# A decoder trunk on one core: the first input projection in two passes of four k-tiles, silu(c) without its last copies, half of the first squares on VectorE

## The chip, the cores and the metric

The kernel runs on one core of one Trainium2 chip. The metric is the device time in microseconds (us) of one execution; less is better. The engines that matter are TensorE (PE in the profile; its weight loads are PEld), VectorE (DVE), ScalarE (ACT) and the queue of SyncE (SPq), from which nearly all transfers are issued. Each engine has its own list of instructions, written by a scheduler when the kernel is built.

## What is computed

Two layers of a hybrid decoder for 256 tokens of width 2048, all in float32. The part that matters here is the start: the conditioning c goes through silu and a large matrix and gives, for each layer, shifts, scales and gates; x is normed and modulated with them, and the first (even) layer projects the result to 5120 columns.

```python
cond = jax.nn.silu(c.astype(F32))
for layer in range(DEPTH):
    mod = cond @ ada_w[layer].astype(F32) + ada_b[layer].astype(F32)
    sh1, sc1, g1, sh2, sc2, g2 = jnp.split(mod, 6, axis=-1)
    h = modulate(rmsnorm(x, norm_mix[layer]), sh1, sc1)
    if layer % 2 == 0:
        y = even_mixer(h, positions, ...)      # proj = h @ w_in, then attention and RG-LRU
    else:
        y = odd_mixer(h, positions, ...)
    x = x + (g1[:, None] * y.astype(F32)).astype(x.dtype)
    ...                                        # gated conv FFN, in the same way
return rmsnorm(x, norm_final)
```

`modulate` is h * (1 + scale) + shift.

## The kernel before

Activations are held transposed, as 16 k-tiles of 128 features by 256 tokens. Weights stream from HBM through six buffers of 128x2048 (`w`, also used by the modulation columns), in one queue.

**Products.** For float32 accuracy a weight tile is split: ScalarE casts it to the rounded `hi` (L379 in `slab`, L330 in `pieces`), VectorE subtracts and gives `lo` (L380, L331); there are four buffers of each. The activation is split in the same way, and a product is three: hi by high, hi by low, lo by high. A native form without a split exists as well (`full` in `slab`).

**Modulation.** `ada_tile` (L217) loads one 128x2048 piece of the matrix and reduces it with cond on VectorE (L221): one column of 128 shifts or scales. A k-tile needs two. `modulator` (L298) asks for them in `tile_of` (`ada_upto`), finishes scale and shift by two tiny operations (L310, L311), multiplies x by scale and norm (L289, VectorE), and adds the shift on ScalarE (L291 for the high half, L293 for the native tile), then VectorE makes the low half (L294). Besides the columns that are asked for, `ada_fill` adds columns by a quota after each slab. The columns have a lower priority than other work of the scheduler (`U_ADA`).

**Norm.** `rms` (L258) squares the 16 tiles on ScalarE (L264), sums them by products with ones, and takes root (L280) and reciprocal (L284). silu(c) is made in four pieces of 512: a product that spreads c, tanh (L210, ScalarE), a product on VectorE (L211) and a copy times 0.5 (L212, ScalarE).

**The first projection.** Three slabs, ev_a (v and part of q and k: 7 banks of PSUM), ev_b (7 banks) and ev_c (6 banks), each run by `run` in `slab_set` (L488) over k-tiles 0 to 7; ev_a is native there. As there are eight banks, a slab's banks are copied away by ScalarE (L506) before the next can use them. Then ev_a goes over k-tiles 8 to 15 (L719) and its banks are added on VectorE to what was copied (L509); the rest of ev_b and ev_c, k-tiles 8 to 15, comes in groups of 256 columns (`ev_rest`, L720 on; products of `group`), added in L517. The quotas in `EV_FIRST` (L40) are the columns per k-tile for the three slabs.

Of the kernel before, what the change touches and what calls it, by code (L numbers as in the profile page):

```python
# [14 lines left out]
AF = mybir.ActivationFunctionType  # L15
# [4 lines left out]
D = 2048  # L20
# [19 lines left out]
EV_FIRST = (0.0, 0.6, 1.0)  # L40
# [55 lines left out]
def trunk(ctx: ExitStack, tc: tile.TileContext, a: dict, out: bass.AP):  # L96
# [54 lines left out]
    def pin():  # L151
        """the next product comes after all the products before it"""
        pinned[0] = PIN

    def start(chain, prio=0):
        """a chain of work whose parts go between pieces of the weight stream"""
        chains.append((chain, prio))
        advance(chains[-1])
# [15 lines left out]
    # ---------------------------------------------------------------- inputs that are needed first  # L174
# [28 lines left out]
    # silu(c), the same row on all partitions  # L203
    cond = cst.tile([P, D], F32, name="cond")
    for h in range(4):
        c = slice(h * 512, (h + 1) * 512)
        ps = pss()
        mm(ps, ones[0:1, :], crow[:, c], True, True)
        th = t2()
        S.activation(th, ps, AF.Tanh, scale=0.5)  # L210
        V.scalar_tensor_tensor(th, th, 1.0, ps, op0=ALU.add, op1=ALU.mult)  # L211
        S.activation(cond[:, c], th, AF.Copy, scale=0.5)  # L212

    # ---------------------------------------------------------------- adaLN: one column of 128 at a time
    mods = [cst.tile([P, 96], F32, name=f"mods{l}") for l in range(2)]

    def ada_tile(l, j):  # L217
        w = sb.tile([P, D], F32, tag="w", name=nm("ada"), bufs=WB)
        DMA.dma_start(w, a["adaT"][l, j])
        with urgent(U_ADA):  # L220
            V.tensor_tensor_reduce(out=w, in0=w, in1=cond, scale=1.0, scalar=0.0, op0=ALU.mult,  # L221
                                   op1=ALU.add, accum_out=mods[l][:, j:j + 1])
# [19 lines left out]
    def gate_of(l, q):  # L242
        """gate(i): columns i and i + 1 of a gate"""
# [13 lines left out]
    # ---------------------------------------------------------------- norm  # L257
    def rms(on_pe=False, warm=(0, 0)):  # L258
        """1 / sqrt(mean(x^2) + eps); warm: products that only keep the array's clock up, before the sum and after"""
        ps = pss()  # L260
        acc = None
        for i in range(KT):
            sq = t1()
            S.activation(sq, x[i], AF.Square)  # L264
# [33 lines left out]
    def modulator(l, q, g, on_pe=False):  # L298
        """h[i](): the i-th k-tile of the normed and modulated x; q: the chunk of the shift"""
# [21 lines left out]
    # ---------------------------------------------------------------- weight streams  # L321
# [13 lines left out]
    def group(srcs, acts):  # L335
        """out^T of 256 columns: [128, 2, T] in one bank; srcs: (chunk, k-tiles)."""
# [18 lines left out]
    def group_f32(src, acts):  # L355
        """the same, with float32 operands that are not split"""
# [10 lines left out]
    def slab(src, n, xa, first, last, pv, pg, full=None):  # L367
        """one k-tile of n columns: of v (token-major: pv[2 * half + block]) and of groups of 256"""
# [14 lines left out]
        def product(o, wide, cs, bs, st):  # L383
            """wide: the weights are the moving operand"""
# [19 lines left out]
    def step(emit, post, quota, when=False, prio=0):  # L404
        """a group's products come before the last group's results are used"""
# [19 lines left out]
    def out_proj(name, g0, gate, acts, quota, chunked=False, base=None):  # L425
        """x += gate * (acts @ W) for all 2048 columns; chunks from g0 on.
        Without a gate x becomes the product alone; with a base it holds such a product, and base the old x."""
# [37 lines left out]
    # ---------------------------------------------------------------- sin and cos of an angle  # L465
# [6 lines left out]
    def sin_cos1(sn, cm, ang):  # L472
        """sn = sin(ang), cm = cos(ang) - 1; ang in [-pi, pi]"""
# [4 lines left out]
    # ---------------------------------------------------------------- start: ada of layer 0, tables  # L478
# [9 lines left out]
    def slab_set(specs, tile_of):  # L488
        """specs: (name, columns, banks of v, groups); run(si, k0, k1, ..): the k-tiles k0..k1 of one of them"""
# [22 lines left out]
        def rest(si, g, k0, post, quota):  # L512
            """group g of a slab without v: its k-tiles from k0 on"""
# [14 lines left out]
    for si in range(3):  # L528
        ev_slab(si, 0, HALF, EV_FIRST[si], si == 0)
# [17 lines left out]
    def rope(o, src, tab, half, by_dma=False):  # L547
        """o, src: [128, n, T]"""
# [14 lines left out]
    # softplus(-lambda) = max(-lambda, 0) + log1p(exp(-|lambda|))  # L563
# [24 lines left out]
    # ---------------------------------------------------------------- S5: what the parameters give  # L588
# [11 lines left out]
    # ---------------------------------------------------------------- attention  # L600
# [41 lines left out]
    # ================================================================ layer 0: mixer  # L642
# [24 lines left out]
    def lru1(i, x2, xin):  # L667
        """gates of tile i; x2: (b, t, a) in the making"""
# [71 lines left out]
    # ================================================================ FFN  # L740
# [64 lines left out]
    # ================================================================ layer 1: mixer  # L805
# [88 lines left out]
    def s5_load(g, ps):  # L894
        """two tiles of u: rows (t, 32 channels) -> (q, 32 channels)"""
# [12 lines left out]
    def turn_rows(src, dst, g):  # L908
        """[128 (a, 32), m, b, c] -> [128 (b, 32), m, a, c]"""
# [15 lines left out]
    def s5_all():  # L925
        """tile i's tables, tile i - 1's states and tile i - 2's outputs, side by side"""
# [63 lines left out]
    # ================================================================ last norm  # L990
# [9 lines left out]
# -------------------------------------------------------------------- S5  # L1000
# Chunks of 4 tokens; 64 chunks. In a chunk, with A = exp(lam dt) and Bb = ((A - 1) / lam) B:
#   v_c = sum_j A^(3-j) Bb u_(4c+j),  H_c = A^4 H_(c-1) + v_c,
#   y_(4c+j) = Re(C A^(j+1) H_(c-1)) + sum_(d<=j) Re(C A^d Bb) u_(4c+j-d) + D u_(4c+j).
# H is scanned in a frame that turns with A^4, where the decay is real.
# [344 lines left out]
```

## Time and profile before

| | |
|---|---|
| time, median of 3 runs | 2273.1 us |
| lowest and highest run | 2271.8 and 2273.46 us |
| span of the profiled execution | 2271.8 us |
| TensorE busy | 2209.5 us (97%) |
| VectorE busy | 1812.8 us (80%) |
| ScalarE busy | 1221.4 us (54%) |
| HBM | 269 GB/s over the span |

The profiled execution's own time is its span. A busy TensorE means that a product is in the pipe; a product's row also holds its way through the array, so rows of a stream overlap, and the distance from start to start tells what one costs. The same holds, with less overlap, for VectorE. "Idle before" names what ended an engine's idle time just before an instruction.

### The profile page before, as it was taken

The numbers are of one execution on the slowest core, as the hardware profiler recorded it, in microseconds if no ns is written. First come the engines' busy times: TensorE is split into PE (matmuls) and PEld (weight loads), VectorE is DVE, ScalarE is ACT, GpSimd is POOL, SyncE is SP. The second block draws the span as 40 slices with busy tenths as digits, with TensorE's granted clock in tenths as the row PEclk, the third lists the DMA queues.
The fourth block names the chain that finished last, engine by engine and source line by source line (L and its number), as shares of the span: only waits on it lengthen the run. The fifth ranks groups of instructions, "written<-read, shape, count | busy, mean of one in ns | idle before, by whom it ended". The sixth has DMA issues, their size and how long they took to land. (4 is left out here: it accounts for less than half of the span.)

```text
span 2271.8 us, 42923 instructions
## 1 busy us (share of the span) xinstructions
PE 2209.5 (97%) x17498; PEld 2148.6 (95%) x17498; DVE 1812.8 (80%) x2908; ACT 1221.4 (54%) x2056; POOL 4.4 (0%) x12
## 2 busy tenths in 40 slices
PE   7999999998999999999999999999999999999997
PEld 4899989898999999999999899999999999999997
DVE  7789989989998869989778778986888657666655
ACT  3355856444775456654445767644565434544543
POOL 0000000000000000000000000000000000000000
PEclk9999999999999999999999999999999999999998
DMA  9988689888669778888866665967756667655541
GB/s 349 373 337 308 235 303 350 333 327 338 259 242 352 306 295 317 320 336 314 304 238 224 245 254 224 342 222 289 276 181 222 238 244 287 234 185 180 203 181 69
DMA packets 106088, 615.43 MB, mean 271 GB/s; under 512 B 12065, under 2 KB 14625, under 8 KB 54817
## 3 DMA queue, kind: packets, MB, share of 16 engines
q1 hardware_dynamic: 105890, 612.69, 71.9%
q8 instruction: 137, 2.24, 0.4%
q14 instruction: 61, 0.50, 0.1%
HBM read 592.72 MB, written 18.87 MB: 269 GB/s over the span
## 5 line engine op out<-in xcount | busy, mean ns | idle before, releaser
L138 PE MATMUL mm<-t,hi 128*128 128x256 f32 x9568 | 1744.2, 284 | 7.3 <-ACT hi L379 4.3
L138 PEld LDWEIGHTS mm<-t,hi 128*128 128x128 f32 x9568 | 1498.5, 193 | 10.4 <-ACT hi L379 4.7
L138 PE MATMUL mm<-t,lo 128*128 128x256 f32 x4784 | 1356.7, 284 | 5.1 <-DVE lo L331 5.1
L138 PEld LDWEIGHTS mm<-t,lo 128*128 128x128 f32 x4784 | 919.8, 192 | 7.3 <-DVE lo L331 5.8
L330 ACT CAST hi<-w 128x1024 fp32r<-128x1024 f32 (+1 forms) x558 | 565.4, 1016 | 594.4 <-PE mm L138 523.2
L331 DVE TENSOR_TENSOR lo<-w,hi 128x1024 fp32r<-128x1024 f32 (+1 forms) x558 | 657.5, 1182 | 280.2 <-ACT hi L330 276.3
L221 DVE CUSTOM_DVE_ANT_0 ada<-ada,cond 128x2048 f32<-128x2048 f32 x192 | 438.3, 2283 | 22.7 <-DMA ada<-in_adaT 19.7
L379 ACT CAST hi<-w 128x768 fp32r<-128x768 f32 (+2 forms) x160 | 146.4, 921 | 163.1 <-PE sx L138 86.6
L380 DVE TENSOR_TENSOR lo<-w,hi 128x768 fp32r<-128x768 f32 (+2 forms) x160 | 167.4, 1061 | 62.3 <-ACT hi L379 61.6
L138 PE MATMUL sp<-t,hi 128*128 128x256 f32 x832 | 153.6, 283 | 0.0
L138 PEld LDWEIGHTS sp<-t,hi 128*128 128x128 f32 x832 | 130.3, 192 | 0.8 <-ACT hi L379 0.2
L138 PE MATMUL sp<-t,lo 128*128 128x256 f32 x416 | 117.1, 283 | 0.0
L759 DVE SCALAR_TENSOR_TENSOR t<-mm,ffn_p,t 128x255 f32<-128x255 f32 x232 | 110.6, 477 | 4.2 <-ACT t L757 1.7
L138 PEld LDWEIGHTS sp<-t,lo 128*128 128x128 f32 x416 | 79.6, 192 | 0.1
L291 ACT ACTIVATE t<-t,mods 128x256 fp32r<-128x256 f32 x64 | 30.0, 505 | 85.6 <-DVE mods L311 62.8
L138 PE MATMUL sx<-t,t 128*128 128x64 f32 (+2 forms) x480 | 68.3, 283 | 3.3 <-DMA t<-s 1.1
L757 ACT ACTIVATE t<-mm,ffn_p 128x256 f32<-128x256 f32 x116 | 65.0, 560 | 5.6 <-DVE t L759 5.4
L138 PEld LDWEIGHTS sx<-t,t 128*128 128x128 f32 x480 | 61.5, 194 | 5.9 <-issue 3.3
L264 ACT ACTIVATE t<-x 128x256 f32<-128x256 f32 x80 | 31.9, 414 | 59.4 <-DVE x L451 31.9
L138 PE MATMUL mm<-t,w 128*128 128x256 f32 x256 | 56.5, 379 | 0.9 <-ACT t L665 0.9
L138 PEld LDWEIGHTS mm<-t,w 128*128 128x128 f32 x256 | 48.5, 190 | 7.8 <-ACT t L665 1.3
L318 ACT CAST t<-t 128x256 fp32r<-128x256 f32 x102 | 40.2, 402 | 26.1 <-DVE t L763 20.1
(264 smaller groups left out, 1475.1 us busy)
## 6 DMA issues: line engine op xcount, KB each, us to landing
ada<-in_adaT SPq DMA_DIRECT2D x192, 1024.0 KB, 6.5
w<-in_ffn_in SPq DMA_DIRECT2D x116, 1024.0 KB, 6.1
w<-in_ffn_out SPq DMA_DIRECT2D x80, 896.0 KB, 4.7
w<-in_ffn_first SPq DMA_DIRECT2D x48, 896.0 KB, 6.6
w<-in_ev_out SPq DMA_DIRECT2D x16, 1024.0 KB, 6.4
w<-in_ffn_out SPq DMA_DIRECT2D x16, 1024.0 KB, 5.2
w<-in_od_out SPq DMA_DIRECT2D x16, 1024.0 KB, 7.4
w<-in_ev_a SPq DMA_DIRECT2D x16, 896.0 KB, 7.0
```

The source lines that it names most:

```text
L138: keep(PE.matmul(o, l, r, start=start, stop=stop, skip_group_check=True))
L221: V.tensor_tensor_reduce(out=w, in0=w, in1=cond, scale=1.0, scalar=0.0, op0=ALU.mult, op1=ALU.add, accum_out=mods[l][:, j:j + 1])
L264: S.activation(sq, x[i], AF.Square)
L291: S.activation(o[:, 0, :], t, AF.Identity, bias=sh[:, i:i + 1])
L318: S.copy(o[:, 0, :], src)
L330: S.copy(hi[:, :m], w[:, o:o + m])
L331: V.tensor_tensor(lo[:, :m], w[:, o:o + m], hi[:, :m].bitcast(F32), op=ALU.subtract)
L379: S.copy(hi[:, :c], w[:, o:o + c])
L380: V.tensor_tensor(lo[:, :c], w[:, o:o + c], hi[:, :c].bitcast(F32), op=ALU.subtract)
L757: S.activation(c, ps[:, s, :], AF.Identity, bias=fp[:, 3, j:j + 1], scale=fp[:, 2, j:j + 1])
L759: V.scalar_tensor_tensor(c[:, d:], ps[:, s, :T - d], fp[:, 2 - d, j:j + 1], c[:, d:], op0=ALU.mult, op1=ALU.add)
```

## The change

The three slabs go over k-tiles 0 to 3 first, and then, in a second round, over 4 to 7. In `run` a slab that doesn't start at k-tile 0 adds its banks on VectorE (L511 in the changed kernel, which is L509 here), so the second round adds 20 banks; the number of copies on ScalarE stays 20. Only k-tiles 0 to 3 of ev_a are native now (`si == 0 and k0 == 0`). The quotas are 0, 1, 1 columns per k-tile in the first round and 0.6 in the second. The copy times 0.5 behind silu(c) goes away and the 0.5 goes into the reduction of the columns. The squares of odd tiles of the first norm are made by VectorE. All else in the difference are comments that are left out and lines that move by two or three.

```diff
-EV_FIRST = (0.0, 0.6, 1.0)
+EV_FIRST = ((0, 4, (0.0, 1.0, 1.0)), (4, 8, (0.6, 0.6, 0.6)))
...
         S.activation(th, ps, AF.Tanh, scale=0.5)
-        V.scalar_tensor_tensor(th, th, 1.0, ps, op0=ALU.add, op1=ALU.mult)
-        S.activation(cond[:, c], th, AF.Copy, scale=0.5)
...
+        V.scalar_tensor_tensor(cond[:, c], th, 1.0, ps, op0=ALU.add, op1=ALU.mult)
...
-            V.tensor_tensor_reduce(out=w, in0=w, in1=cond, scale=1.0, scalar=0.0, op0=ALU.mult,
+            V.tensor_tensor_reduce(out=w, in0=w, in1=cond, scale=0.5, scalar=0.0, op0=ALU.mult,
                                    op1=ALU.add, accum_out=mods[l][:, j:j + 1])
...
         for i in range(KT):
             sq = t1()
-            S.activation(sq, x[i], AF.Square)
+            if on_pe and i % 2:
+                V.tensor_tensor(sq, x[i], x[i], op=ALU.mult)
+            else:
+                S.activation(sq, x[i], AF.Square)
...
-    for si in range(3):
-        ev_slab(si, 0, HALF, EV_FIRST[si], si == 0)
+    for k0, k1, quotas in EV_FIRST:
+        for si in range(3):
+            ev_slab(si, k0, k1, quotas[si], si == 0 and k0 == 0)
```

Three places of VectorE's list show what moves. In the names, ada is a piece of the modulation matrix, mods the columns, x the four blocks of x, sp and sm small parameters, t a tile. An ada row is followed by a row that reads its sum out into mods.

The first excerpt is VectorE at the start, ahead of the first column. Before:

```order
L211 SCALAR_TENSOR_TENSOR t_8_101<-t_8_101,sp_99 128x512
L580 TENSOR_SCALAR sp_1281<-sp_1281 128x8
L1026 TENSOR_SCALAR sm_1316<-sm_1316 128x32
L1027 SCALAR_TENSOR_TENSOR sm_1315<-sm_1316,pack 128x32
L1028 SCALAR_TENSOR_TENSOR sm_1315<-sm_1316,sm_1315 128x32
L1029 TENSOR_SCALAR sm_1315<-sm_1315 128x32
L1030 TENSOR_SCALAR sm_1316<-sm_1316 128x32
L1031 CAST sm_1317<-sm_1316 128x32
L221 ISA ada_171,mods_105<-ada_171,cond 128x2048
L221 ISA mods_105 128x1
```

and after the change:

```order
L1031 SCALAR_TENSOR_TENSOR sm_1440<-sm_1441,sm_1440 128x32
L575 TENSOR_TENSOR sp_1407<-sp_1405,sp_1408 128x8
L1032 TENSOR_SCALAR sm_1440<-sm_1440 128x32
L576 TENSOR_TENSOR sp_1408<-sp_1407 128x8
L264 TENSOR_TENSOR t_25_149<-x_73 128x256
L577 TENSOR_SCALAR sp_1405<-sp_1408 128x8
L1033 TENSOR_SCALAR sm_1441<-sm_1441 128x32
L579 TENSOR_TENSOR sp_1405<-sp_1405,sp_1408 128x8
L1034 CAST sm_1442<-sm_1441 128x32
L220 ISA ada_167,mods_101<-ada_167,cond 128x2048
```

The last product of silu(c) (L211) stood eight rows ahead of the first column and now stands further ahead; the square of the last tile (L264 here) stands five rows ahead of the column.

The second excerpt is VectorE in the last eight k-tiles of ev_a. Before, one column stands behind the weights of k-tile 12 and the low half of k-tile 14's activation (t_277_1753):

```order
L311 TENSOR_TENSOR mods_105<-mods_105,pack 128x1
L289 SCALAR_TENSOR_TENSOR t_276_1751<-x_73,A_160,t_27_158 128x256
L380 TENSOR_TENSOR lo_1662<-w_1659,hi_1661 128x1024
L380 TENSOR_TENSOR lo_1666<-w_1659,hi_1665 128x768
L294 SCALAR_TENSOR_TENSOR t_277_1753<-t_276_1751,mods_105,t_277_1753 128x256
L221 ISA ada_1699,mods_105<-ada_1699,cond 128x2048
L221 ISA mods_105 128x1
L310 SCALAR_TENSOR_TENSOR A_160<-mods_105,b_29_161,pack 128x1
L289 SCALAR_TENSOR_TENSOR t_284_1801<-x_73,A_160,t_27_158 128x256
L303 TENSOR_SCALAR b_639_4006<-pack 128x16
```

and after the change three columns stand in a row behind the weights of k-tile 11 and ahead of the low half of its activation (t_281_1731):

```order
L382 TENSOR_TENSOR lo_1737<-w_1734,hi_1736 128x1024
L382 TENSOR_TENSOR lo_1741<-w_1734,hi_1740 128x768
L220 ISA ada_1677,mods_101<-ada_1677,cond 128x2048
L220 ISA mods_101 128x1
L220 ISA ada_1774,mods_101<-ada_1774,cond 128x2048
L220 ISA mods_101 128x1
L313 TENSOR_TENSOR mods_101<-mods_101,pack 128x1
L220 ISA ada_1777,mods_101<-ada_1777,cond 128x2048
L220 ISA mods_101 128x1
L296 SCALAR_TENSOR_TENSOR t_281_1731<-t_280_1729,mods_101,t_281_1731 128x256
```

From here to k-tile 15 two columns stand ahead of each modulated tile, nine in all; before, four were spread over the eight k-tiles.

The third excerpt is VectorE at the end of these k-tiles, where the additions of ev_a's banks (mm, sx, sp) and the first chunk of ev_b's rest meet. Before, the low half of the chunk's first part (lo_1857) stands ahead of the additions:

```order
L294 SCALAR_TENSOR_TENSOR t_285_1803<-t_284_1801,mods_105,t_285_1803 128x256
L380 TENSOR_TENSOR lo_1809<-w_1806,hi_1808 128x1024
L380 TENSOR_TENSOR lo_1813<-w_1806,hi_1812 128x768
L331 TENSOR_TENSOR lo_1857<-w_1854,hi_1856 128x1024
L509 TENSOR_TENSOR t_85_386<-mm_1451,t_85_386 128x512
L331 TENSOR_TENSOR lo_1861<-w_1854,hi_1860 128x1024
L509 TENSOR_TENSOR t_86_387<-mm_1452,t_86_387 128x512
L509 TENSOR_TENSOR t_87_388<-mm_1453,t_87_388 128x512
```

and after the change it (lo_2000) stands behind all of them and behind a column:

```order
L382 TENSOR_TENSOR lo_1953<-w_1946,hi_1952 128x768
L511 TENSOR_TENSOR t_61_274<-mm_1576,t_61_274 128x512
L220 ISA ada_1986,mods_101<-ada_1986,cond 128x2048
L220 ISA mods_101 128x1
L511 TENSOR_TENSOR t_62_275<-mm_1577,t_62_275 128x512
L511 TENSOR_TENSOR t_63_276<-mm_1578,t_63_276 128x512
L511 TENSOR_TENSOR t_64_277<-sx_1579,t_64_277 128x512
L511 TENSOR_TENSOR t_65_278<-sp_1580,t_65_278 128x512
L511 TENSOR_TENSOR t_66_279<-sp_1581,t_66_279 128x512
L511 TENSOR_TENSOR t_67_280<-sp_1582,t_67_280 128x512
L333 TENSOR_TENSOR lo_2000<-w_1997,hi_1999 128x1024
```

What moved is the low half of the next weights: from ahead of the first addition to behind the seventh.

## Rows read from the trace of the kernel before

**Rows 1.** Section 1 of the page: busy us (share of the span) xinstructions.

```profile
PE 2209.5 (97%) x17498; PEld 2148.6 (95%) x17498; DVE 1812.8 (80%) x2908; ACT 1221.4 (54%) x2056; POOL 4.4 (0%) x12
```

**Rows 2.** By stretch: us, busy PE, PEld, DVE, ACT, POOL; PEclk; DMA share; GB/s.

```profile
25.10:34.40 9.30, 9.28 (x21) 5.15 (x22) 8.83 (x45) 4.03 (x7) 0.00 (x0) 0.67 0.94 348
51.10:59.00 7.90, 7.89 (x21) 4.54 (x22) 7.22 (x10) 0.91 (x2) 0.00 (x0) 0.78 0.93 364
84.10:124.40 40.30, 40.30 (x337) 40.27 (x336) 29.29 (x33) 19.06 (x25) 0.00 (x0) 1.00 0.93 352
124.40:159.30 34.90, 34.88 (x291) 34.68 (x289) 30.69 (x42) 14.11 (x21) 0.00 (x0) 1.00 0.96 382
159.30:202.70 43.40, 39.83 (x240) 35.43 (x241) 38.26 (x55) 22.05 (x31) 0.00 (x0) 1.00 0.81 310
202.70:242.70 40.00, 39.79 (x328) 39.36 (x327) 39.26 (x83) 28.54 (x47) 0.00 (x0) 1.00 0.63 225
...
160.30:196.00 35.70, 33.12 (x195) 29.22 (x196) 33.08 (x48) 18.20 (x27) 0.00 (x0) 1.00 0.80 312
```

**Rows 3.** Timeline of PE: start, us, line, operation, count, [idle before <- what ended it].

```profile
25.12 5.49 PE L138 MATMUL mm<-w,t 128*128 128x512 f32 x6 [5.42 <-ACT t L293]
...
51.11 4.54 PE L138 MATMUL mm<-w,t 128*128 128x512 f32 x6 [2.99 <-ACT t L293]
...
58.94 2.74 PE L138 MATMUL mm<-w,t 128*128 128x512 f32 x6
...
64.96 2.74 PE L138 MATMUL mm<-w,t 128*128 128x512 f32 x6
```

**Rows 4.** Groups of VectorE, 16 to 200 us: count | busy us, mean ns | idle before.

```profile
L221 DVE CUSTOM_DVE_ANT_0 ada<-ada,cond 128x2048 f32<-128x2048 f32 x32 | 73.1, 2284 | 3.9 <-ACT cond L212 2.8 <-DMA ada<-in_adaT 1.1
...
L294 DVE SCALAR_TENSOR_TENSOR t<-t,mods,t 128x256 fp32r<-128x256 f32 x16 | 7.5, 480 | 7.3 <-ACT t L291 7.3
...
L470 DVE SCALAR_TENSOR_TENSOR t<-t,t 128x256 f32<-128x256 f32 x3 | 1.2, 416 | 0.0
```

**Rows 5.** Timeline of VectorE, single rows from 13 to 203 us.

```profile
13.39 0.18 DVE L1031 CAST sm<-sm 128x32 int32<-128x32 f32 x1
16.39 2.29 DVE L221 CUSTOM_DVE_ANT_0 ada<-ada,cond 128x2048 f32<-128x2048 f32 x1 [2.82 <-ACT cond L212]
...
50.69 0.48 DVE L294 SCALAR_TENSOR_TENSOR t<-t,mods,t 128x256 fp32r<-128x256 f32 x1 [0.57 <-ACT t L291]
...
132.93 1.83 DVE L380 TENSOR_TENSOR lo<-w,hi 128x1024 fp32r<-128x1024 f32 x2
...
160.34 0.48 DVE L294 SCALAR_TENSOR_TENSOR t<-t,mods,t 128x256 fp32r<-128x256 f32 x1 [3.85 <-ACT t L291]
...
169.60 4.09 DVE L380 TENSOR_TENSOR lo<-w,hi 128x1024 fp32r<-128x1024 f32 x4
...
195.01 0.95 DVE L380 TENSOR_TENSOR lo<-w,hi 128x768 fp32r<-128x768 f32 x1
...
202.27 1.87 DVE L509 TENSOR_TENSOR t<-sp,t 128x512 f32<-128x512 f32 x3
```

**Rows 6.** Timeline of ScalarE: the last copy of silu(c).

```profile
15.75 0.61 ACT L212 ACTIVATE cond<-t 128x512 f32<-128x512 f32 x1
```

**Rows 7.** Timeline of PE where ev_a's last k-tiles begin, and where the next chunk does.

```profile
161.69 1.65 PE L138 MATMUL mm<-hi,t 128*128 128x512 f32 x6 [2.41 <-ACT hi L379]
...
202.74 0.40 PE L138 MATMUL mm<-t,hi 128*128 128x256 f32 x2
202.98 0.28 PE L138 MATMUL mm<-t,lo 128*128 128x256 f32 x1
```

**Rows 8.** DMA issues, 0 to 200 us: count, KB each, median us to landing.

```profile
ada<-in_adaT SPq DMA_DIRECT2D x34, 1024.0 KB, 6.8
...
w<-in_ev_b SPq DMA_DIRECT2D x8, 896.0 KB, 7.9
w<-in_ev_c SPq DMA_DIRECT2D x8, 768.0 KB, 6.2
```

## The prediction

> **What bounds the kernel now.** I read first the busy line of the page: TensorE works 97% of the span and VectorE 80% [rows 1]. So what the change gives must come from TensorE work that disappears or from the 3% in which TensorE waits, and what it costs can come from VectorE becoming late. Second, the table by stretch [rows 2]: from 84.1 to 159.3 TensorE is full; the stretch from 159.3 to 202.7, in which the last eight k-tiles of ev_a run, has a hole of 3.6 us. VectorE is the other full engine: 8.83 of 9.30 us near the start, 38.26 of 43.40 in the last eight k-tiles, 39.26 of 40 after that. Third, the start on TensorE [rows 3]: k-tile 0 begins at 25.12 behind a wait of 5.42, k-tile 3 at 51.11 behind 2.99, both for ScalarE's modulated tile; from k-tile 4 at 58.94 the native float32 k-tiles follow each other every 6.02 us, and ev_b begins at 84.1. Fourth, what VectorE does there [rows 4, 5]: 32 modulation columns ("ada", 2.28 us each, two per k-tile), the low halves of the split weights, and the modulated tiles. The first column starts at 16.39, and the last operation for k-tile 3 at 50.69; the table shows hardly any idle time between. So k-tile 3 waits for VectorE's list, not for TensorE.
>
> **The sum goes by VectorE's list.** VectorE works its instructions off in the order in which they stand, so I follow that list from the first column to the weights of ev_b's rest. The three excerpts of the order are the fixed points, and TensorE waits where it must.
>
> **Start.** Removed: four copies of silu(c) on ScalarE; the last starts at 15.75, takes 0.61 us, and the first column starts behind it at 16.39 [rows 5, 6]. Added: eight squares on VectorE. No row of before shows one; the nearest are operations on 128x256 of 0.42 to 0.48 us [rows 4, 5]. They don't put 8 x 0.45 on the path, since VectorE stood idle for 2.82 us ahead of 16.39, but the last square waits until TensorE's sum has read the eighth, and it stands nearly directly ahead of the first column (first excerpt). I take the first column at 15.2; the bounds are 13.6, when the small operation of 13.39 is done, and 16.4. From there to k-tile 3 the list has 113 instructions where 119 stood, tiny ones at 0.1 us: 0.5 less. So k-tile 3 starts at about 51.1 - 1.7 = 49.4, and ends at 57.2 if it takes 7.8 us as before (51.11 to 58.94), of which 1.8 are the lower clock.
>
> **The two passes on TensorE.** K-tiles 4 to 7 of ev_a leave the native form: 6.02 us each [rows 3] become three products of split halves, which take 41.05 / 8 = 5.1 us, short waits included (161.69 to 202.74) [rows 7]. That is the gain: 3.7 us. An ev_b tile is 40.3 / 8 = 5.04 us and an ev_c tile 34.9 / 8 = 4.36 [rows 2]. Behind k-tile 3 follow 20.2 (ev_b), 17.4 (ev_c), 20.4 (ev_a), 20.2 and 17.4: 95.6 us, to 152.8 without a wait. I add three waits. ScalarE has five evictions ahead of the first cast of ev_c: 0.3. In ev_c's first pass two tiles take VectorE 2 x (2.3 + 1.8) for columns and low halves [rows 4, 5] and 0.8 to 1.0 for the modulation, 9.0 to 9.2, against 8.7 on TensorE: 1.1 in all. From ev_c to ev_a the first cast stands behind the last eviction and one modulation, 0.6 + 0.5 + 1.0 = 2.1, close to the 2.41 that the trace shows at a border of the same kind [rows 7]. Together 156.3, where 159.3 stood: 3.0 us earlier.
>
> The second pass adds its banks on VectorE instead of copying them on ScalarE: 20 additions of some 0.62 us [rows 5], 12.4 us of new VectorE work, and four k-tiles of ev_a now need low halves, 4 x 2.0 = 8 [rows 5]. The first two borders hide this: a bank is finished several products before the next slab wants it, and VectorE's list for a slab of four tiles (halves 8, additions 4.3, two or three columns 4.6 to 6.9) sums to 17 to 19 us against 20. At the third border VectorE is late by itself: going through its list I find it done with ev_c's six additions at 157.4. Before, the same point (the first low half of an activation of the last eight tiles) is 160.34 [rows 5].
>
> **The last eight k-tiles of ev_a.** Here the sign is decided. All 32 columns must be done by k-tile 15, before and after. Before, 16 are done in the first ev_a, 12 more by the quotas 0.6 x 8 + 1.0 x 8, and 4 stand in this stretch. After: 8, then 1.0 x 8 = 8, then 0.6 x 12 = 7; 9 are left to stand here (second excerpt: three of them ahead of one low half). VectorE's list of before takes 160.3 to 196.0, 35.7 us, of which 33.1 are busy [rows 2, 5]. After: 35.7 + 5 x 2.3 (columns) + 0.4 (one more product with the norm) + 0.7 (rope's angle, partly done earlier before) + 0.5 (five tiny operations) + 1.7 (three more waits of 0.57 for ScalarE, like the one at 50.69) - 1.5 (waits for casts, which are no longer last) = 49.0 us. TensorE needs 41. The list ends at 157.4 + 49.0 = 206.4, where before it ends at 195.01 + 0.95 = 196.0.
>
> Behind it the order changes once more (third excerpt). Before, the low half of the next chunk stands ahead of the additions, and TensorE goes on at 202.74 without a hole. After, there come an addition, a column, six additions and only then that low half: 0.6 + 2.3 + 3.7 + 1.2 = 7.8. The first product with it starts at 214.2, against 202.98 [rows 7]: **11.2 us later**. TensorE's last k-tile, 205 to 210, or to 212 at a lower clock, hides in that.
>
> Beyond it the list is the same. By the output projection 40 columns are done in both, so one column less (2.3 us) stands in a stretch in which TensorE loses 0.2 us of 40 [rows 2]; I give it nothing (bounds 0 and -2.3). The profiled execution spans 2271.8 us, which is also the lowest of the three runs; the median is 2273.1. On the span the sum gives 2283.0, on the median **2284.3 us**.
>
> **Clock.** Two waits in the start are followed by half speed: behind the 5.42 us before k-tile 0 the granted clock is 0.67 over 25.1 to 34.4, and the tile takes 9.3 instead of 6.02; behind the 2.99 us before k-tile 3 it is 0.78, and the tile takes 7.8; behind 2.41 us at 159.3 it stays at 1.00 [rows 2, 3, 7]. In the last eight tiles I expect TensorE to wait about 5 us in tile 11 and 3 to 4 us in 14 and 15. The loss would be 3.3 + 1.8 + 1.8 = 6.9 if nothing hid it; since what follows waits for VectorE anyway I count 0, and keep 6.9 for the range. The Trainium skill, "TensorE: Matmul & The Clock Gate", section "HAM oscillation — how this bites in real kernels", speaks against the change: it advises to run all k-tiles of an output in one go, since waits between the pieces let the clock fall. By it the 6.9 would be paid in full; the drops at 25.1 and 51.1 agree that waits do this, and no run here shows whether a late VectorE hides the price.
>
> **Rivals.** *Faster*: TensorE alone decides. It is 3.0 us ahead at the end of ev_c, 6.5 if the three waits don't come, and the stretch costs 43.4 as before: 2266 to 2270, say 2268. For it: TensorE is 97% busy and loses 3.7 us of work. Against it: VectorE's list would have to fit in the some 41 us of the stretch, so it decides at one or two columns more than the four of before; the order has five more. 5%. *No change*: the passes run better than I count: no waits (-3.5), full clock in k-tile 3 (-1.8), first column at 13.6 (-1.6). The last list then starts near 151 and ends near 200; about +4, 2277. 10%. *Worse*: DMA and clock. The first pass behind k-tile 3 needs 8 columns of 1024 KB, 4 tiles of 896 and 4 of 768 [rows 8], 15.2 MB, in 37.6 us: 404 GB/s, where the stretches show 348 to 382 [rows 2]; at 382 it takes 2.2 us more, at 352 5.6. With part of the 6.9 of clock: +14 to +23, say 2291. 14%. That the forecast holds (2280 to 2289): 71%.
>
> **How the numbers follow.** A difference of 0.2%, 4.5 us, is about what can be told from none. Faster by that: 5%. Within it: the middle rival and an edge of the forecast, 11%. Slower: 84%. The range takes in most of the two slower rivals: 2276 to 2294.
>
> **What would show it.** Right: TensorE finishes k-tile 3 at 55 to 58 and the passes at 154 to 158; the last eight tiles of ev_a take 50 us or more, with TensorE waiting for low halves of activations or weights while VectorE has no idle time and nine columns there; the first products of ev_b's rest wait for their low half behind the additions. Wrong: VectorE with idle time in that stretch, a start of the last eight tiles before 150, or TensorE waits there that end with a DMA.

## The result and the profile after

The changed kernel takes 2284.8 us (median of 4 runs, 2279.6 to 2291.9) against 2272.45 us for the kernel before on the same chip: a ratio of 1.0055, 95% interval 1.0032 to 1.0078. It is slower by about 12 us, by the interval 7 to 18; the prediction said 2284.3. The profiled execution is the fastest of the four: span 2277.9, time 2279.64 us, 1.7 us above its span. The 2271.8 us of the profiled execution of the kernel before is a span as well, so the 2277.9 is to be compared with it: 6.1 us more.

The busy line of the page, answering to [rows 1]: TensorE is busy 1.7 us longer, VectorE 21.5.

```profile
PE 2211.2 (97%) x17538; PEld 2152.1 (94%) x17538; DVE 1834.3 (81%) x2944; ACT 1222.5 (54%) x2048; POOL 4.4 (0%) x12
```

The table by stretch of the changed kernel, with the columns of [rows 2]: the first k-tile, k-tile 3, the last eight k-tiles of ev_a with the wait behind them, and the 40 us after that.

```profile
25.60:34.40 8.80, 8.72 (x20) 4.87 (x21) 8.13 (x30) 3.85 (x7) 0.00 (x0) 0.69 0.80 292
52.40:58.30 5.90, 5.90 (x19) 3.72 (x20) 1.90 (x3) 4.46 (x8) 0.00 (x0) 1.00 0.88 333
156.70:213.00 56.30, 45.46 (x244) 38.05 (x242) 54.01 (x78) 19.37 (x28) 0.00 (x0) 0.94 0.90 337
213.00:253.00 40.00, 39.53 (x322) 38.96 (x323) 39.23 (x80) 27.03 (x44) 0.00 (x0) 1.00 0.69 243
```

The third row is where the time goes: 56.3 us, where before 43.4 stood, with VectorE busy for 54.0 of them and TensorE for 45.5.

TensorE's timeline of the changed kernel at the same places as [rows 3] and [rows 7]:

```profile
25.68 5.49 PE L138 MATMUL mm<-w,t 128*128 128x512 f32 x6 [6.39 <-ACT t L295]
...
52.40 2.84 PE L138 MATMUL mm<-w,t 128*128 128x512 f32 x6 [0.98 <-ACT t L295]
...
58.34 0.59 PE L138 MATMUL mm<-t,hi 128*128 128x256 f32 x2
...
175.10 0.98 PE L138 MATMUL mm<-hi,t 128*128 128x512 f32 x3 [2.30 <-ACT t L293]
...
194.51 2.63 PE L138 MATMUL mm<-hi,t 128*128 128x512 f32 x6 [3.48 <-ACT hi L381]
...
203.59 0.73 PE L138 MATMUL mm<-hi,t 128*128 128x512 f32 x2 [2.31 <-ACT hi L381]
...
213.27 0.50 PE L138 MATMUL mm<-t,hi 128*128 128x256 f32 x2 [1.88 <-ACT hi L332]
```

The reader is to see that k-tile 0 does not start earlier than before (25.12), that k-tile 3 is done at 58.34 (before 58.94), and that three long waits stand in the last eight k-tiles and one behind them. The last row is the place of the 202.98 of [rows 7]: 213.27, 10.3 us later (the record of the first product with the low half is missing in this trace; this row is the first one behind the wait). The releasers named are ScalarE's, but ScalarE itself waits for VectorE there, for a shift (mods) three times and for an addition at the end:

```profile
174.54 0.51 ACT L293 ACTIVATE t<-t,mods 128x256 fp32r<-128x256 f32 x1 [5.83 <-DVE mods L313]
...
193.02 0.51 ACT L293 ACTIVATE t<-t,mods 128x256 fp32r<-128x256 f32 x1 [7.28 <-DVE mods L313]
...
202.09 0.51 ACT L293 ACTIVATE t<-t,mods 128x256 fp32r<-128x256 f32 x1 [6.90 <-DVE mods L313]
...
210.90 1.25 ACT L560 COPY t<-t 64x512 f32<-64x512 f32 x2 [4.74 <-DVE t L511]
```

VectorE's timeline shows what it does meanwhile:

```profile
157.73 0.48 DVE L296 SCALAR_TENSOR_TENSOR t<-t,mods,t 128x256 fp32r<-128x256 f32 x1
...
169.93 2.28 DVE L220 CUSTOM_DVE_ANT_0 ada<-ada,cond 128x2048 f32<-128x2048 f32 x1
172.14 0.08 DVE L220 DVE_READ_ACCUMULATOR2_ANT mods<- 128x1 f32 x1
172.14 2.28 DVE L220 CUSTOM_DVE_ANT_0 ada<-ada,cond 128x2048 f32<-128x2048 f32 x1
174.36 0.08 DVE L220 DVE_READ_ACCUMULATOR2_ANT mods<- 128x1 f32 x1
174.36 0.15 DVE L313 TENSOR_TENSOR mods<-mods,pack 128x1 f32<-128x1 f32 x1
174.43 2.28 DVE L220 CUSTOM_DVE_ANT_0 ada<-ada,cond 128x2048 f32<-128x2048 f32 x1
...
205.58 0.68 DVE L511 TENSOR_TENSOR t<-mm,t 128x512 f32<-128x512 f32 x1
206.18 2.28 DVE L220 CUSTOM_DVE_ANT_0 ada<-ada,cond 128x2048 f32<-128x2048 f32 x1
...
210.18 1.87 DVE L511 TENSOR_TENSOR t<-sp,t 128x512 f32<-128x512 f32 x3
211.98 2.35 DVE L333 TENSOR_TENSOR lo<-w,hi 128x1024 fp32r<-128x1024 f32 x2
```

Of the three columns in a row from 169.93, two stand ahead of the shift (L313, 174.36) that ScalarE waits for: they are the wait of 2.30 at 175.10; the third stands ahead of the low half of the same activation (L296, 176.64) and holds TensorE up for another 0.50. One addition, a column, six additions and then the low half are the wait at 213.27.

**One ledger for all kernels.** The end of k-tile 3 differs from execution to execution (57.0 to 62.2 us), also between kernels that are the same up to there; the cause is open. So I compare the distance D from the end of k-tile 3 (58.94 before, 58.34 after) to the first product that needs the next chunk's low half (202.98 and 213.27): 144.0 us before, 154.9 after. VectorE's groups in this distance, before and then after (count | busy us, mean ns | idle before):

```profile
L221 DVE CUSTOM_DVE_ANT_0 ada<-ada,cond 128x2048 f32<-128x2048 f32 x22 | 50.2, 2284 | 1.1 <-DMA ada<-in_adaT 1.1
L380 DVE TENSOR_TENSOR lo<-w,hi 128x1024 fp32r<-128x1024 f32 (+2 forms) x48 | 48.9, 1043 | 18.1 <-ACT hi L379 17.8
```

```profile
L220 DVE CUSTOM_DVE_ANT_0 ada<-ada,cond 128x2048 f32<-128x2048 f32 x25 | 57.0, 2284 | 0.0
L382 DVE TENSOR_TENSOR lo<-w,hi 128x1024 fp32r<-128x1024 f32 (+2 forms) x55 | 55.8, 1045 | 6.9 <-ACT hi L381 6.9
L511 DVE TENSOR_TENSOR t<-mm,t 128x512 f32<-128x512 f32 x12 | 7.9, 685 | 1.7 <-PE mm L138 1.7
L511 DVE TENSOR_TENSOR t<-sp,t 128x512 f32<-128x512 f32 x11 | 7.2, 686 | 0.1
L511 DVE TENSOR_TENSOR t<-sx,t 128x512 f32<-128x512 f32 x4 | 2.7, 686 | 0.0
```

And the whole of it, before and after, as rows of the table by stretch:

```profile
58.94:202.90 143.96, 139.41 (x947) 125.57 (x946) 116.43 (x155) 62.48 (x87) 0.00 (x0) 1.00 0.91 354
```

```profile
58.34:213.00 154.66, 141.38 (x988) 130.95 (x986) 143.22 (x192) 64.54 (x88) 0.00 (x0) 0.98 0.90 340
```

VectorE's busy time grew by 26.8 us (143.22 - 116.43). It is additions (27 here, 13.8 us more than in the same distance before; 20 of them are the second round's), seven of the eight new low halves (6.9), and three columns (6.8: the one at 206.18, and two that before had been done ahead of k-tile 3's end); as rows overlap, these groups add up to a little more. Its idle time fell from 27.5 to 11.4, and the distance grew by 10.7. TensorE's busy time is the same within 2 us.

### The profile page after: what moved, and what is told of

Read it like the earlier page. It is cut to its first block, busy times and chain, and to the rows that moved or that the text cites. A ratio compares the mean times of both kernels' runs of the same rounds, so it can differ in the third digit from the quotient of the medians.

```text
span 2277.9 us, 43038 instructions
## 1 busy us (share of the span) xinstructions
PE 2211.2 (97%) x17538; PEld 2152.1 (94%) x17538; DVE 1834.3 (81%) x2944; ACT 1222.5 (54%) x2048; POOL 4.4 (0%) x12
## 5 line engine op out<-in xcount | busy, mean ns | idle before, releaser
L381 ACT CAST hi<-w 128x1024 fp32r<-128x1024 f32 (+2 forms) x168 | 153.4, 922 | 161.4 <-PE sx L138 83.6
L382 DVE TENSOR_TENSOR lo<-w,hi 128x1024 fp32r<-128x1024 f32 (+2 forms) x168 | 175.8, 1063 | 54.4 <-ACT hi L381 53.9
L138 PE MATMUL sp<-t,hi 128*128 128x256 f32 x880 | 162.7, 283 | 0.0
L138 PEld LDWEIGHTS sp<-t,hi 128*128 128x128 f32 x880 | 138.1, 191 | 1.2
L138 PE MATMUL sp<-t,lo 128*128 128x256 f32 x440 | 123.8, 283 | 0.0
L762 DVE SCALAR_TENSOR_TENSOR t<-mm,ffn_p,t 128x255 f32<-128x255 f32 (+1 forms) x232 | 110.7, 478 | 3.7 <-ACT t L760 1.3
L762 DVE SCALAR_TENSOR_TENSOR t<-t,ffn_p,t 128x255 f32<-128x255 f32 (+1 forms) x112 | 49.5, 476 | 3.0 <-ACT t L760 3.0
```

The lines of the kernel that those rows point to most:

```text
L138: keep(PE.matmul(o, l, r, start=start, stop=stop, skip_group_check=True))
L381: S.copy(hi[:, :c], w[:, o:o + c])
L382: V.tensor_tensor(lo[:, :c], w[:, o:o + c], hi[:, :c].bitcast(F32), op=ALU.subtract)
L762: V.scalar_tensor_tensor(c[:, d:], ps[:, s, :T - d], fp[:, 2 - d, j:j + 1], c[:, d:], op0=ALU.mult, op1=ALU.add)
```

## The experiments

Each run gives a time beside runs of the kernel before on the same chip (medians of before: 2273.0 to 2273.5 us), and one profile. The table has what the profiles say: D as above, and how much later than before the product at its end starts.

| kernel | median us | ratio, 95% interval | D us | product, against 202.98 |
|---|---|---|---|---|
| before | 2272.5 | | 144.0 | |
| changed | 2284.8 | 1.0055, 1.0032 to 1.0078 | 154.9 | +10.3 |
| changed, again | 2287.7 | 1.0059, 1.0044 to 1.0074 | 155.0 | +10.0 |
| new order alone | 2280.7 | 1.0034, 1.0022 to 1.0047 | 155.0 | +9.5 |
| silu and squares alone | 2276.0 | 1.0013, 1.0004 to 1.0022 | 144.5 | +0.2 |
| silu alone | 2275.4 | 1.0003, 0.9994 to 1.0012 | 145.5 | -0.5 |
| squares alone | 2272.2 | 0.9996, 0.9986 to 1.0005 | 145.1 | +0.6 |
| 1 column per k-tile | 2287.1 | 1.0063, 1.0048 to 1.0078 | 153.6 | +12.9 |
| no additions | 2285.3 | 1.0057, 1.0042 to 1.0073 | 155.4 | +11.7 |
| ev_a native in both rounds | 2287.4 | 1.0067, 1.0050 to 1.0084 | 153.2 | +8.7 |
| the same, columns beside ev_a | 2276.5 | 1.0010, 1.0001 to 1.0020 | 147.9 | +5.8 |
| short columns at the end | 2271.9 | 0.9996, 0.9986 to 1.0005 | 143.0 | +0.3 |
| low half first | 2283.8 | 1.0049, 1.0032 to 1.0066 | 153.2 | +10.4 |
| before, with columns left | 2276.9 | 1.0018, 1.0007 to 1.0029 | 144.3 | -0.7 |

**The order alone.** The kernel before with this edit only:

```diff
-EV_FIRST = (0.0, 0.6, 1.0)
+EV_FIRST = ((0, 4, (0.0, 1.0, 1.0)), (4, 8, (0.6, 0.6, 0.6)))
...
-    for si in range(3):
-        ev_slab(si, 0, HALF, EV_FIRST[si], si == 0)
+    for k0, k1, quotas in EV_FIRST:
+        for si in range(3):
+            ev_slab(si, k0, k1, quotas[si], si == 0 and k0 == 0)
```

> The new order of the slabs alone; silu(c) and the first squares as in the kernel before. Theory (VectorE's list in the last eight k-tiles of ev_a decides): the order carries the whole loss, and the edits of silu(c) and the squares bring nothing, since k-tile 0 starts at 25.7 in the changed kernel against 25.1 before. So 2282 to 2287 us, within 2 us of the changed kernel, and the first product with the next chunk's low half about 10 us later than before. Rival (the squares on VectorE make the start late and this is handed on to the end of the list): 2 to 4 us faster than the changed kernel, 2280 to 2282.

In the trace the whole loss is there: D is 155.0 as in the changed kernel. By time it is 8 us slower than before, and 4 to 7 us below the two medians of the changed kernel, which is the rival's band and not the theory's. As the product at the end of D is only 0.5 to 0.8 us earlier than in the changed kernel, the rival's reason, the start, does not explain these microseconds; they lie behind it. The traced executions do not show them: the span is 2278.5 here, 2277.9 and 2280.4 in the changed kernel's two (see the clock, below).

**The other two edits alone**, in the order of before (`cond` written by the product on VectorE, 0.5 in the reduction, odd squares on VectorE):

> The order of the slabs as before; silu(c) without its last copies and the odd first squares on VectorE. Theory (these edits are hidden at the start or worth little): 2271 to 2273 us, within 1.5 us of the kernel before; k-tile 0 does not start earlier than 24.5. Rival (they are a gain of about a microsecond at the first column, as forecast, that the start hands on undiminished): 2269 to 2271. Rival (the squares put VectorE in the way of the start): 2273.5 to 2276.

The product stands where it stood, 0.2 us later. The time is 3 us longer, by interval 0.9 to 5.0: above the theory's band and at the end of the second rival's. But the rival's reason, a late start, is not in the trace: k-tile 0 starts at 25.57, and none of the 3 us is seen in the first 300 us. With the order's 7.7 they make 10.7 of the changed kernel's 12.3 and 14.6; as each of the two edits by itself (below) costs nothing that can be told, what makes these 3 us stays open.

**The changed kernel again:**

> The changed kernel once more, unaltered. Its four runs lay between 2279.6 and 2291.9 us, with a granted clock that went from .988 to .980 as the time went up. Theory (VectorE's list costs 8 to 10 us in every run, and half-speed stretches behind the new waits add 0 to 8 more): again a scatter of some 10 us with the time following the clock, in a trace the first low half of the next chunk at about the same place within 2 us, and TensorE's half-speed stretches in other places. Rival (the scatter belongs to that one chip and job): all runs within 3 us.

The scatter came again: 2282.2, 2286.9, 2288.4, 2288.6 us at a mean granted clock of 0.986, 0.984, 0.985, 0.983. D is the same to 0.1 us.

**More columns in the second round:**

```diff
-EV_FIRST = ((0, 4, (0.0, 1.0, 1.0)), (4, 8, (0.6, 0.6, 0.6)))
+EV_FIRST = ((0, 4, (0.0, 1.0, 1.0)), (4, 8, (1.0, 1.0, 1.0)))
```

> The changed kernel with 1 column per k-tile in the second round in place of 0.6: 28 columns are done before the last eight k-tiles of ev_a, 4 are left there, as before, and the next chunk's low half stands ahead of the additions again. Theory (VectorE's total work decides: the five columns only move forward into the second round, where VectorE has 1 to 3 us to spare per slab, not 11): ev_a's last eight k-tiles start 3 to 7 us later, end 3 to 6 us earlier than in the changed kernel, 2278 to 2282 us. Rival (only where the columns stand decides): the whole loss goes, 2272 to 2275.

Only where the columns stand does not decide. The last eight k-tiles now run at TensorE's pace (42.1 us), but they begin 17 us later (13 if counted from the end of k-tile 3), behind this wait:

```profile
173.68 2.06 PE L138 MATMUL mm<-hi,t 128*128 128x512 f32 x3 [6.20 <-ACT t L293]
```

D is 1.3 us shorter, less than the 3 to 6 that I had given it, and the median, 2287.1, is outside both bands: VectorE had no room in the second round (142.1 of 153.6 us of D busy here).

**The additions left out:**

```diff
-                    V.tensor_tensor(o, b, o, op=ALU.add)
+                    k1 == HALF or V.tensor_tensor(o, b, o, op=ALU.add)
```

> The changed kernel without the 20 additions of the second round: the products of the second round are made and dropped, so what k-tiles 4 to 7 give to the projection is left out. It takes 20 x 0.6 = 12.4 us off VectorE, 8.6 of it beside the first two slabs of the round, where VectorE has time to spare, and 3.7 at the third border, directly ahead of the last list. Theory (VectorE's list counts from ev_c's additions on): the last eight k-tiles start 2 to 4 us earlier and the next chunk's low half comes 3 to 6 us earlier, 2279 to 2283 us with the scatter of the clock. Rival (the nine columns alone are the loss; the additions are hidden): within 2 us of the changed kernel.

The rival holds: 20 additions are gone, VectorE's busy time in D falls from 143.2 to 132.8 us, and D is 0.5 us longer. So the sum of VectorE's work alone does not set D. VectorE does not use the room, since no columns are put there; it waits 18.0 us for casts. From k-tile 12 on it then has two columns per k-tile, and such a k-tile takes 9.0 us on VectorE, with two short waits for ScalarE, where TensorE needs 5.1:

```profile
188.88 2.29 DVE L220 CUSTOM_DVE_ANT_0 ada<-ada,cond 128x2048 f32<-128x2048 f32 x1
...
191.87 2.28 DVE L220 CUSTOM_DVE_ANT_0 ada<-ada,cond 128x2048 f32<-128x2048 f32 x1
...
194.93 0.48 DVE L296 SCALAR_TENSOR_TENSOR t<-t,mods,t 128x256 fp32r<-128x256 f32 x1 [0.57 <-ACT t L293]
195.86 2.09 DVE L382 TENSOR_TENSOR lo<-w,hi 128x1024 fp32r<-128x1024 f32 x2 [0.45 <-ACT hi L381]
197.87 2.29 DVE L220 CUSTOM_DVE_ANT_0 ada<-ada,cond 128x2048 f32<-128x2048 f32 x1
```

From column to column of the next k-tile it is 188.88 to 197.87.

**ev_a native in both rounds**, with 1 column per k-tile:

```diff
-            ev_slab(si, k0, k1, quotas[si], si == 0 and k0 == 0)
+            ev_slab(si, k0, k1, quotas[si], si == 0)
```

> The changed kernel with k-tiles 4 to 7 of ev_a native again (no low halves there: 4 x 2 = 8 us less of VectorE) and 1 column per k-tile in the second round. TensorE pays 3.7 us for the native tiles. Theory (the sum of VectorE's work up to the last eight k-tiles decides): the five columns now fit into the room of the 8 us, four are left at the end as in the kernel before, the next chunk's low half comes 5 to 9 us earlier than in the changed kernel, 2274 to 2280 us. Rival (the waits of the modulation chain and the clock are the loss, not VectorE's work): no better than with 1 column per k-tile alone, 2284 or more, and 3.7 us more for the native products.

Eight us of low halves less bring 1.7 us of D, and only 0.4 against the run with 1 column per k-tile, from which this one differs in nothing else. The time, 2287.4, is in the rival's band. VectorE stands idle beside the native slab: three of the quota's four columns there are done by 107.7, the next in its list is an addition that waits for TensorE's bank, and VectorE is late afterwards:

```profile
116.63 0.69 DVE L511 TENSOR_TENSOR t<-mm,t 128x512 f32<-128x512 f32 x1 [8.89 <-PE mm L138]
```

**The same with the columns put into that hole**, 2 per k-tile beside ev_a, and 0.6 beside the other two:

```diff
+EV_FIRST = ((0, 4, (0.0, 1.0, 1.0)), (4, 8, (2.0, 0.6, 0.6)))
```

> The changed kernel with k-tiles 4 to 7 of ev_a native again, and in the second round 2 columns per k-tile beside ev_a and 0.6 beside ev_b and ev_c: 8 + 8 + 8 + 4 = 28 columns are done before the last eight k-tiles, 4 are left, and the columns are put where VectorE makes no low halves and no additions. Theory (TensorE waits for the sum of VectorE's work, and VectorE's room beside a native slab is the room that the change gave up): the list is done about as in the kernel before, the product that the changed kernel starts 9 to 10 us late is at most 3 us late, 2272 to 2278 us. Rival (two rounds cost the loss by themselves, by their additions and borders): 5 us late or more, 2280 or more.

D falls to 147.9, 7.0 us less than in the changed kernel, and the time to 2276.5, 8 to 11 us less. VectorE is busy for the same time in D as in the run before this one (134.3 and 134.5 us), and D is 5.3 us shorter: here the place of the work decides, not its sum. The product still starts 5.8 us late, more than the 3 that I had allowed and within the rival's 5 or more; 1.9 of them are a later end of k-tile 3 (60.85). The time lies in the theory's band, near its upper end. The 3.9 us that D is still longer than before are not explained.

**Short columns.** The nine columns left for the end are reduced over 256 of their 2048 rows:

```diff
+            n = 256 if 23 <= ada_done[0] < 32 else D
-            V.tensor_tensor_reduce(out=w, in0=w, in1=cond, ...
+            V.tensor_tensor_reduce(out=w[:, :n], in0=w[:, :n], in1=cond[:, :n], ...
```

> The changed kernel with the nine columns that are left for the last eight k-tiles of ev_a reduced over 256 of their 2048 rows (the rest of their sums is left out): all transfers, waits and instructions stay, but each takes about 0.4 us of VectorE in place of 2.28, some 17 us less. Theory (VectorE's time in that list is what TensorE waits for): the waits of 2.3 and 3.5 us in the stretch go, it takes 41 to 44 us, and the kernel comes to 2271 to 2277 us, near or below the kernel before. Rival (the transfers of the columns or the turn of hands between ScalarE and VectorE per tile decide, not VectorE's busy time): the waits stay above 2 us and the time above 2281.

All of the loss goes: D is 143.0. VectorE's busy time in D falls by more than the loss, from 143.2 to 125.4 us, so the run shows that VectorE's time is what counts there, and not what one column costs. The transfers and the turns between the engines are still there, but a column takes 0.42 us. VectorE goes through a k-tile in 5.3 to 7.7 us, and waits for ScalarE's casts and for transfers now:

```profile
181.09 2.10 DVE L383 TENSOR_TENSOR lo<-w,hi 128x1024 fp32r<-128x1024 f32 x2 [0.46 <-ACT hi L382]
...
185.51 0.43 DVE L221 CUSTOM_DVE_ANT_0 ada<-ada,cond 128x256 f32<-128x256 f32 x1 [1.21 <-DMA ada<-in_adaT]
...
188.79 2.09 DVE L383 TENSOR_TENSOR lo<-w,hi 128x1024 fp32r<-128x1024 f32 x2 [1.59 <-ACT hi L382]
```

**The low half first**, by a priority of 1000 for the first low half of the first chunk (the edit gives it to that one only). In the trace it stands behind four of the seven additions, ahead of the last three:

> The changed kernel with a higher priority for the first low half of each chunk: at the end of ev_a's last eight k-tiles the next chunk's low half stands behind three of the seven additions rather than behind all. Theory (the first product with it waits for VectorE's list at 213.3 us): 1.5 to 2.5 us of the loss go there, 2281 to 2286 us; with the scatter of the clock it may not be told from the changed kernel by time, but the first product with that low half starts at about 211 to 212 in the trace. Rival (TensorE's own last k-tile or its banks hold it up anyway): the start stays within 0.7 us.

D is 1.7 us shorter, as forecast. The product itself starts at 213.4 and not at 211 to 212, because k-tile 3 ended 1.8 us later in that execution; by the start alone the rival would hold, and it is D that speaks against it. The time cannot be told from that of the changed kernel.

**Columns left, without the second round.** The kernel before with other quotas:

```diff
-EV_FIRST = (0.0, 0.6, 1.0)
+EV_FIRST = (0.0, 0.5, 0.375)
```

> The kernel before, in its one round, with the quotas 0, 0.5 and 0.375 in place of 0, 0.6 and 1: 23 or 24 of the 32 columns are done before the last eight k-tiles of ev_a, and 8 or 9 are left to stand there, as in the changed kernel; no second round, no additions of it, no low halves in the first four slabs, no edit of silu(c) or the squares. Theory (the columns that are left there are enough for the loss): VectorE's list of the stretch grows by 4 to 5 columns of 2.37 us, part of it into the 2.6 us in which it stood idle; from the end of k-tile 3 to the first product with the next chunk's low half 6 to 10 us more than the 144.0 of before; 2278 to 2284 us. Rival (the two rounds are needed for it: VectorE comes late into the stretch by their additions and low halves): less than 4 us more, 2272 to 2277.

My theory falls in this form. Eight columns stand in the last eight k-tiles, four more than before, the next low half stands behind all seven additions as in the changed kernel, and D is 144.3. VectorE's time from 159.3 to 196.0, before and then here (the whole of it, and the columns):

```profile
159.30:196.00 36.70, 33.12 (x195) 29.22 (x196) 33.08 (x48) 19.20 (x29) 0.00 (x0) 1.00 0.81 314
```

```profile
159.30:196.00 36.70, 35.40 (x214) 31.61 (x215) 36.51 (x51) 17.07 (x24) 0.00 (x0) 1.00 0.94 378
L221 DVE CUSTOM_DVE_ANT_0 ada<-ada,cond 128x2048 f32<-128x2048 f32 x8 | 18.2, 2283 | 0.0
```

Of the 9.1 us that four columns take, 3.4 went into idle time; the rest is other work (low halves, modulated tiles, rope's angle) that VectorE had done before 159.3, in the room that the missing columns left in ev_b and ev_c. VectorE is full here, 36.51 of 36.70 us: the run shows that four more columns cost nothing, and not that the changed kernel's ten ahead of the low half (nine, and the one at 206.18) would cost nothing. The 3.8 us by which the median is longer (by interval 1.6 to 6.6) are not in D; the traced execution has a mean clock of 0.985 where before has 0.988.

**The two small edits, each alone:**

> The kernel before with silu(c) without its last copies, and nothing else. Theory (the squares on VectorE, which wait for TensorE's sum, stand ahead of the first column and eat the gain): without them the first column starts at 13.5 to 15.5 us instead of 16.4 and k-tile 0 at 23.5 to 24.8 instead of 25.1; k-tile 3, bound by VectorE's list, 1 to 2 us earlier; 2270 to 2273 us. Rival (ScalarE's root of the norm decides k-tile 0, and the list hands on nothing): k-tile 0 and k-tile 3 within 0.3 us of before, 2272 to 2274.

> The kernel before with the odd first squares on VectorE, and nothing else. Theory (these squares are the harm in the start): the first column starts 0.5 to 1.5 us later than before, at 16.9 to 17.9, and k-tile 0 at 25.5 to 26.5; 2273 to 2277 us. Rival (they make the sum of squares end earlier and k-tile 0 with it): k-tile 0 at 24.0 to 25.0, 2271 to 2273.

Neither theory nor rival is right in the start. Without the squares the first column does not come at 13.5 to 15.5: the order puts operations on small parameters ahead of it, and one of these waits for ScalarE. Two rows of the kernel with silu alone:

```profile
15.81 0.18 DVE L1032 TENSOR_SCALAR sm<-sm 128x32 f32<-128x32 f32 x1 [1.37 <-ACT sm L1031]
...
16.30 2.23 DVE L220 CUSTOM_DVE_ANT_0 ada<-ada,cond 128x2048 f32<-128x2048 f32 x1
```

And with the squares alone the column starts at 16.47, not at 16.9 or later. K-tile 0 starts at 25.7 and 25.3. By time neither can be told from before.

## Why the prediction came out right, step by step

**Start: wrong.** The first column was put at 15.2, between 13.6 and 16.4; it starts at 16.85. These are rows of VectorE at the start of the changed kernel:

```profile
14.14 0.42 DVE L264 TENSOR_TENSOR t<-x 128x256 f32<-128x256 f32 x1 [1.05 <-PE sp L138]
...
16.14 0.42 DVE L264 TENSOR_TENSOR t<-x 128x256 f32<-128x256 f32 x1
...
16.85 2.28 DVE L220 CUSTOM_DVE_ANT_0 ada<-ada,cond 128x2048 f32<-128x2048 f32 x1
```

The squares wait for TensorE's sum in VectorE's list, and the small operations behind them are held up with them. The prediction saw the last square ahead of the column and still gave a gain. K-tile 3 began at 52.4 and not at 49.4, but took 5.9 us at full clock and not 7.8, so its end, 58.3 against 57.2, was off by 1.1 only: two errors that nearly cancel, by luck.

**The passes: right.** ev_a's last k-tiles begin at 156.70 (156.3), ev_c's additions are done at 157.6 (157.4). From the end of k-tile 3 to the start of ev_a's last k-tiles TensorE is busy 95.9 us where before it was 99.4: 3.5 us less (3.7). The 20 additions were taken at 0.62: a row is 0.686 us long, but in a stream they follow each other every 0.60 (208.38, 209.59, 210.18), so they cost about 12.1 us (12.4).

**The last list: right in place and size.** From 157.6 to 205.66 it takes 48.1 us (49.0), with nine columns, and the low half behind it ends 7.5 us later (7.8). The product starts 10.3 us late (11.2). TensorE's waits were put at 5 us in k-tile 11 and 3 to 4 in 14 and 15; they are 2.30, 3.48 and 2.31. The signs that were named came: the stretch takes over 50 us, with nine columns and 2.3 us without VectorE work in 56.3; only k-tile 3 ended at 58.3 instead of by 58.

**The reason behind the list: half right.** The prediction priced each column that is left at 2.3 us on the list of before, and let VectorE decide at one or two columns more than the four of before. The short columns bear out that VectorE's time for the columns at the end is what TensorE waits for. But the kernel of before with eight columns there, four more, loses nothing in D. My reading is that the columns cost only because the second round leaves VectorE no room to get ahead: additions and low halves fill it (D's ledger), and in the run without additions the room is there but nothing is put into it. That fits all runs and is not shown by one of them: the run that would decide it, no additions and more columns together, was not tried. What is shown is that columns put into the room beside a native slab win back 7.0 of the 10.9 us of D, where the native slab without them wins back 1.7.

**The later column: taken at 0, and nothing shows more.** From 257 to 340 us the lag of the changed kernel falls from 10.5 to 8.6 us, from 11.7 to 10.9 in its second profile, and from 11.2 to 9.3 with the order alone. But there the kernels with silu alone and with the squares alone, whose columns are those of before, gain as well: the product that before starts at 258.26 starts at 257.76 and 258.87 in them, and the one at 336.58 at 335.02 and 336.16, a gain of 1.1 and 1.0 us. In that stretch the traced execution of before has two waits for transfers (0.40 and 0.69 us). At most a microsecond is left for the column.

**The clock: right in the stretch, open in the median.** The waits do bring half speed; the granted clock from 160 to 213 us differs between three executions with the same order (changed, changed again, order alone):

```profile
160.00:213.00 53.00, 42.25 (x228) 35.54 (x227) 50.74 (x72) 18.50 (x26) 0.00 (x0) 0.94 0.92 342
```

```profile
160.00:213.00 53.00, 43.14 (x228) 36.38 (x226) 50.72 (x72) 18.88 (x27) 0.00 (x0) 0.90 0.91 342
```

```profile
160.00:213.00 53.00, 41.36 (x229) 35.31 (x229) 50.73 (x72) 19.34 (x27) 0.00 (x0) 0.94 0.91 347
```

D is 154.9, 155.0 and 155.0 all the same, and VectorE is busy for 50.7 of 53 us in all three. Between 0.94 and 0.90 lie 2.1 us of TensorE's time at full speed (0.04 x 53), and nothing of it is seen in D: half speed is free while VectorE is late. In the Trainium skill, "TensorE: Matmul & The Clock Gate", section "HAM oscillation — how this bites in real kernels", waits between pieces let the clock fall; the trace agrees that it falls (1.00 before, 0.90 to 0.94 here), and not that it is paid for in this stretch.

But the median is 12.3 and in the second job 14.6 us above before, where the traces end at 6.4 and 8.9. What goes with the rest is the clock: the changed kernel's eight runs go from 2279.6 us at a mean clock of 0.988 to 2291.9 at 0.980, before's first 15 from 2271.4 at 0.988 to 2277.6 at 0.984. Its profiled executions are the faster ones. Only they have a trace, so which waits cost the slower runs their clock stays open. So the closeness of the total is partly luck. On the span the sum gave 2283.0 us, and the traced executions have 2277.9 and 2280.4. The product behind the list comes 10.3 and 10.0 us late where 11.2 was forecast, but at 340 us 8.6 and 10.9 are left, and at the end 6.4 and 8.9. The rest of the medians goes with a lower clock, which was counted as nothing; that the clock makes it is argued from these means and not shown.

## What to carry to other kernels

Add up the work that an edit gives to the second busiest engine from the edit on, not in the one stretch where it is seen: here 26.8 us met 27.5 us of idle time, which looked like enough and was not. The sum is only the first question: without the additions VectorE had 10.4 us less to do and D was no shorter, and of two runs with the same work the one that put it where VectorE stood idle was 5.3 us shorter. A surplus shows up where a deadline stands, as work left over (nine columns), far behind the place that was edited; moving it forward helps only into room that is really empty. And while one engine is late, what the engine that waits for it does can cost nothing: half speed was free there.

## What was not expected of the hardware

The four runs of the changed kernel in the first job scatter by 12 us (2279.6 to 2291.9), with a mean granted clock that differs by 0.008. The kernel before scattered less: 2271.4 to 2277.6 in 15 runs on one chip, 2270.9 to 2279.8 in 26 on another. A half of a per cent of difference is then as large as the scatter, and a single run of each kernel could have shown anything from nothing to 20 us.
